# Four edits to the mixer of a hybrid decoder layer: dt in two stacked passes, v in blocks of 512 columns, norm sums as two halves times ones, the state matmul one projection later

## The chip, the cores and the metric

The kernel runs on one core of a Trainium2 chip, as one program that computes a whole decoder layer for one sequence of 256 tokens. The metric is the time of one execution in microseconds (us) on the device. The kernel before takes 869.53 us (median of three runs, 868.91 to 870.09).

## The reference

The layer has three parts in a row: a SwiGLU block, a mixer, and another SwiGLU block, each behind an RMS norm with a shift and a scale that come from a condition vector. The change is in the mixer alone. D is 1024, the sequence T is 256, a chunk is 128 tokens.

```
proj = u @ w_in        # one product for z, xbc, dt, q, k, v, g and two gates
# Mamba-2 (SSD) branch, 4 groups of 8 heads of 64
dt   = softplus(dt_raw + dt_bias)
y_diag = (cb * segsum_exp(a)) @ xdt
chunk_states = einsum(bm, decay_to_end, xdt)       # carried to the second chunk
y_off = cm @ prev_states * exp(a_cs)
yg = ((y_diag + y_off + xs * d_skip) * silu(z)) grouped in 4 groups of 512 channels
y_ssd = rms_normalize(yg) * norm_w                 # mean over 512 channels
# retention branch, 8 heads, key width 128, value width 256
y = ((q k^T) * decay_mask) @ v  (+ the part across chunks)
y_ret = rms_normalize(y) * norm_w * silu(g)        # mean over 256 channels
out = (sigmoid(gate_ssd) * (y_ssd @ w_br_ssd) + sigmoid(gate_ret) * (y_ret @ w_br_ret)) @ w_out
rms_normalize(x) = x * rsqrt(mean(x * x) + 1e-6)
```

## The kernel before

All data are float32, and a large product is made of reduced pieces. Every operand is split into two halves of type fp32r, a type that the tensor engine takes in one pass: hi is the value rounded to that type (a copy on ACT) and lo is what is left (a subtraction on DVE). A product is then three matmuls that add into one PSUM bank, hi·hi, hi·lo and lo·hi: the function `mm3`, lines 137 to 139, which holds most of the tensor engine's time. Small products are done in plain float32, without halves; each such matmul shows in the trace as two records (x2).

Weights come in pieces of 1 MB into four staging buffers (`wst`, filled by SP's DMA queue), are split by `half` (lines 128 and 129, ACT then DVE) into four pairs of buffers `wh` and `wl`, and are used once. Activations u of the layer stand in SBUF as `uh` and `ul`, features on the partitions, tokens along the free axis.

PSUM is used in two pools. **proj** has four banks of 128 x 512 float32, one for each projection under way; **misc** has the other four, for all small products. Nearly every projection takes one proj bank: two halves of 256 tokens, or, in v, two chunks of 128 tokens by 256 columns. A bank is given to the next tile in turn when its reader, a copy or activation on ACT or an addition on DVE, has emptied it.

The mixer is a list of steps, the string ORDER, and each step is one Python function: `dt`, `conv`, `states`, `mul`, `back`, `norma`, `normb`, `v`, `bs`, `rs`, `rv`, `rn` and so on, with the number of a group, tile or head behind the dot. The string sets the order in which the program is written, and that order sets which buffer a tile gets. A scheduler then orders the instructions of each engine by its own estimates of when their inputs are ready, so that small matmuls land among the projection's matmuls. On the chip each engine runs its own list in order and waits on semaphores.

What the change and the steps ahead speak of:

- `dt` (lines 524 to 534): the raw dt of 32 heads. The weights have only 32 columns, so that the 24 matmuls of `mm3` fill 32 of 128 output rows each. A copy on ACT (531) brings the sum to SBUF and two transposes (534) put tokens on the partitions.
- `states.g` (619 to 637): eight transposes (624) turn one group's channels, DVE multiplies them by dt (625, `xd`) and by the decay to the chunk's end (630, `xe`), and in the same step the state matmul (635) multiplies `xe` by `bn`; ACT copies the result to `st` (636). `back.g` (666 to 688) reads `xd`, the masks and `st`.
- The masks `m` of a group are filled by DMAs of POOL's queue (644, 647, step `ml.g`), which wait until `back` of an earlier group has read the buffers, and then by ACT (655, steps `ma.g` and `mb.g`).
- `norma.g` squares and adds (694 to 697), `normb.g` takes the mean over 512 channels in `rstd`: a matmul of a constant matrix filled with 1/512 and the sums, in plain float32 (line 205), and then logarithm, exponential and a correction step. `rn.h` of a retention head does the same with 1/256, after `rv.h` has made the values and their squares.
- `rv.h` (799 to 810): for each of two halves of a head's 256 columns three matmuls of 128 x 128 in plain float32: value chunk 0 with score columns of chunk 0 (804), the same with those of chunk 1 (805), and value chunk 1 (806), which adds to the latter.
- `v.p` (753 to 764), p from 0 to 7: 256 columns of v, with u as the stationary operand; for each chunk of 128 tokens 24 matmuls of 128 x 256 into one half of a proj bank. A copy on ACT (764) empties the bank.
- `bs.g.q` (713 to 731): the SSD branch's output product of a group, two proj banks for each q, which an ACT copy (729, group 0) or a DVE addition (731) empties.

Of the kernel before, what the change touches and what calls it, by code (L numbers as in the profile page):

```python
# [12 lines left out]
F32 = mybir.dt.float32  # L13
F32R = mybir.dt.float32r
# [4 lines left out]
P = 128  # L19
# [19 lines left out]
K_ID, K_TRI, K_M = 0, 128, 256  # L39
K_INV, K_SGN = 640, 641  # L40
N_CONST = 642

# [16 lines left out]
    "br.3.0 gr.1 br.3.1 ada ada gr.3 ada ada ada "  # L59
)  # L60


def constants():
    c = np.zeros((P, N_CONST), np.float32)
    i = np.arange(P)
    c[:, K_ID:K_ID + P] = np.eye(P)
    c[:, K_TRI:K_TRI + P] = i[:, None] <= i[None, :]
    for j, n in enumerate((1024, 512, 256)):
        c[:, K_M + j * P:K_M + (j + 1) * P] = 1.0 / n
    c[:, K_INV] = 10000.0 ** (-(i % 64) / 64.0)  # L70
    c[:, K_SGN] = np.where(i < 64, -1.0, 1.0)
    lg = np.log1p(-np.exp2(-5.0 - np.arange(8)))
    rel = np.arange(T)[None, :] - i[:, None]
    dm = np.where(rel >= 0, np.exp(lg[:, None, None] * np.maximum(rel, 0)), 0.0) * P ** -0.5
    dm = np.ascontiguousarray(dm.transpose(1, 0, 2).reshape(P, 8 * T)).astype(np.float32)
    return c, dm
# [3 lines left out]
def layer(ctx: ExitStack, tc: tile.TileContext, a, out, packing):  # L80
# [60 lines left out]
    def at(pair, *idx):  # L141
        return pair[0][idx], pair[1][idx]
# [8 lines left out]
    triu = k[:, K_TRI:K_TRI + P]  # L151
    mean_m = {n: k[:, K_M + j * P:K_M + (j + 1) * P] for j, n in enumerate((1024, 512, 256))}
    ones = cst.tile([P, P], F32, name="ones")
# [47 lines left out]

    def rstd(parts, n):
        ps = misc_ps()
        for i, s in enumerate(parts):
            pe.matmul(ps[:, :T], mean_m[n], s, start=i == 0, stop=i == len(parts) - 1)  # L205
        rs = sp.tile([P, T], F32, tag="rs", name=nm("rs"), bufs=2)
        t = sp.tile([P, T], F32, tag="rt", name=nm("rt"), bufs=2)
        lookup(rs, ps[:, :T], AF.Ln, bias=epsc)
        lookup(rs, rs, AF.Exp, scale=-0.5)
        dve.tensor_tensor(t, rs, rs, ALU.mult)  # L210
        dve.scalar_tensor_tensor(t, ps[:, :T], EPS, t, ALU.add, ALU.mult)
        dve.tensor_scalar(t, t, -0.5, 1.5, ALU.mult, ALU.add)
        dve.tensor_tensor(rs, rs, t, ALU.mult)
        return rs
# [30 lines left out]
    def modulated(ha, u, jsh, w, cols):  # L245
        rs = []
        ps = early_project(w, cols, u, 1, lambda: rs.append(rstd(sums, D)))
        rs = rs[0]
# [229 lines left out]
    with tc.tile_pool(name="mx", bufs=1, reuse_waits="tile") as mx:  # L478
# [9 lines left out]
        def wide(shape, dt=F32):  # L488
            return mx.tile(shape, dt, tag="m", name=nm("m"), bufs=WIDE_BUFS)
# [34 lines left out]
        def dt_tile():  # L524
            need("e")
            hv = half(load(w_in, 0, KD, C_DT, NH))
            ps = proj_ps()
            for kt in range(KD):
                mm3(ps[:NH, 0, :], at(hv, al, kt), at(u, al, kt), kt == 0, kt == KD - 1)
            dtr = wide([NH, T])  # L530
            act.copy(dtr, ps[:NH, 0, :])
            ps = misc_ps()
            for c in range(2):
                pe.transpose(ps[:, c * NH:(c + 1) * NH], dtr[:, c * P:(c + 1) * P],
                             ident[:NH, :NH])
            v, e, s1, s2, pl = (small([P, 2, NH], n) for n in ("dtv", "dte_", "dts", "dts2", "dtp"))
# [82 lines left out]
        def ssd_states(g):  # L619
            xd = slot([P, 2, 512])  # L620
            for c in range(2):
# [9 lines left out]
                xe.rearrange("p (h q) -> p h q", h=8), xd[:, 0, :].rearrange("p (h q) -> p h q", h=8),  # L631
                dend[:, 8 * g:8 * g + 8].unsqueeze(2).broadcast_to([P, 8, 64]), ALU.mult)
            st = small([P, 512], "st")
            ps = misc_ps()
# [54 lines left out]

        hls = {}  # L690

        def norm_a(g):
            y, sz = xs[g], zs["z", g]
            dve.tensor_tensor(y, y, sz, ALU.mult)
            act.activation(sz, y, AF.Square)
            dve.tensor_tensor(sz[:, 0:2, :], sz[:, 0:2, :], sz[:, 2:4, :], ALU.add)
            dve.tensor_tensor(sz[:, 0, :], sz[:, 0, :], sz[:, 1, :], ALU.add)

        def norm_b(g):
            need("e")  # L700
            y, sz = xs.pop(g), zs.pop(("z", g))
            rs = rstd([sz[:, 0, :]], 512)
            for f in range(4):
# [46 lines left out]

        vn = []

        def v_tile(p2):
            st = load(w_in, 0, KD, C_V + p2 * 256, 256)
            hv = [half(st[:, 4 * i:4 * i + 4, :]) for i in range(2)]
            ps = proj_ps()
            for c in range(2):
                ts = slice(c * P, (c + 1) * P)
                for kt in range(KD):
                    mm3(ps[:, c, :], at(u, al, kt, ts), at(hv[kt // 4], al, kt % 4),  # L760
                        kt == 0, kt == KD - 1)
            if p2 % 2 == 0:
                vn.append(slot([P, 2, 2, T]))
            act.copy(vn[-1][:, p2 % 2], ps)

# [33 lines left out]
        def ret_values(hd):  # L799
            sc, v = scs.pop(hd), vn[hd // 2][:, hd % 2]  # L800
            py = misc_ps().rearrange("p (e t) -> p e t", e=2)
            for eh in range(2):
                es = slice(eh * P, (eh + 1) * P)
                pe.matmul(py[:, eh, :P], v[:, 0, es], sc[:, :P], start=True, stop=True)
                pe.matmul(py[:, eh, P:], v[:, 0, es], sc[:, P:T], start=True, stop=False)
                pe.matmul(py[:, eh, P:], v[:, 1, es], sc[:, T:], start=False, stop=True)
            sq = mx.tile([P, 2, T], F32, tag="cv", name=nm("rsq"), bufs=2)
            act.activation(sq, py, AF.Square)
            dve.tensor_tensor(sq[:, 0, :], sq[:, 0, :], sq[:, 1, :], ALU.add)
            pys[hd] = py, sq  # L810

        def ret_norm(hd):
            need("e")
            py, sq = pys.pop(hd)
            rs = rstd([sq[:, 0, :]], 256)
            y = wide([P, 2, T])
# [14 lines left out]
            "g": lambda g, p2: silu_half(("g", g), C_G + g * 512, p2),  # L831
            "states": ssd_states, "ma": lambda g: ssd_masks(g, 0), "mb": lambda g: ssd_masks(g, 1), "ml": mask_rows,
            "mul": mask_scores, "back": ssd_back, "norma": norm_a,
# [159 lines left out]
```

## Time and profile before

The profiled execution took 870.23 us, at a mean granted TensorE clock of 0.996. Its span, from the first to the last instruction in the trace, is 868.4 us; the other 1.83 us lie around it.

| | before |
|---|---|
| median of 3 runs | 869.53 us (868.91 to 870.09) |
| profiled execution | 870.23 us |
| span of its trace | 868.4 us |
| data moved by DMA | 193.24 MB, mean 223 GB/s |
| casts of weights on ACT, line 128 | 282, 289.3 us busy |
| subtractions on DVE, line 129 | 282, 336.7 us busy |

A row of a timeline reads: start in us from the beginning of the span, busy time in us, engine, line of the kernel, operation, output<-inputs by the program's names, shapes and count, and in brackets the wait just before it and what ended it. Matmuls overlap in the array, so the cost of one in a stream is read from start to start and not from its busy time. PE is TensorE, DVE is VectorE, ACT is ScalarE, POOL is GpSimd.

### The profile page before, as it was taken

Reading aid. Unit: us, or ns where it says so; the run is one execution under the profiler, and the core shown is the slowest. Engines: PE = TensorE matmul, PEld = TensorE weight load, DVE = VectorE, ACT = ScalarE, POOL = GpSimd, SP = SyncE. Lnnn points to the kernel's source line nnn. Section 1 sums busy time; section 2 is a strip of 40 time slices with the busy share of each in tenths; the row PEclk is TensorE's granted clock in tenths of the full one; section 3 lists DMA queues with packets and bytes.
Section 4 is the critical chain, followed back from the end, with each engine's and each line's share of the span. In section 5 each row is a group of like instructions: output and inputs, shape, how many; then the busy total and the mean of one; then the engine's idle time right before and its main releaser. Section 6 shows DMA issues by size and latency. Waiting matters only on the chain.

```text
span 868.4 us, 16684 instructions
## 1 busy us (share of the span) xinstructions
PE 852.7 (98%) x6982; PEld 835.4 (96%) x6982; DVE 667.0 (77%) x1007; ACT 502.5 (58%) x709; POOL 10.3 (1%) x21
## 2 busy tenths in 40 slices
PE   7999999999999999999999999999999999999996
PEld 5999999999999998999999999999999999999896
DVE  6989798986889877788798677976979975455453
ACT  5454444465798686765464558755558644545342
POOL 0000000000100010000000000000000000000000
PEclk9999999999999999999999999999999999999999
DMA  9968878894595454445557664464554784455521
GB/s 362 414 223 334 275 275 321 338 366 183 183 335 193 177 177 176 182 146 178 211 188 276 223 235 159 170 243 146 204 216 171 266 330 172 170 172 180 185 95 48
DMA packets 30589, 193.24 MB, mean 223 GB/s; under 512 B 3489, under 2 KB 3873, under 8 KB 10802
## 3 DMA queue, kind: packets, MB, share of 16 engines
q1 hardware_dynamic: 28658, 186.47, 59.1%
q0 software_dynamic: 1568, 5.28, 1.8%
q8 instruction: 54, 0.88, 0.4%
q10 hardware_dynamic: 288, 0.44, 0.1%
q14 instruction: 21, 0.17, 0.1%
HBM read 191.09 MB, written 1.08 MB: 221 GB/s over the span
## 4 chain that ended last, share of the span: by engine, by line
PE 89%; DVE 5%; ACT 3%; DMA 2%; issue 1%; SPq 0%; DVEq 0%; ACTq 0%
PE proj L139 27%; PE proj L138 27%; PE proj L137 27%; DVE wl L129 2%; PE misc L137 1%; PE misc L139 1%; PE misc L138 1%; PE misc L674 1%; DMA wst<-in_ada_w_dram 1%; PE misc L205 1%; ACT wh L128 1%; DVE wst L181 1%; DMA ada<-in_ada_w_dram 1%; DMA wst<-in_ffn_w_out_dram 1%; PE misc L684 1%
## 5 line engine op out<-in xcount | busy, mean ns | idle before, releaser
L128 ACT CAST wh<-wst 128x1024 fp32r<-128x1024 f32 (+3 forms) x282 | 289.3, 1031 | 275.8 <-PE proj L138 185.4
L129 DVE TENSOR_TENSOR wl<-wst,wh 128x1024 fp32r<-128x1024 f32 (+3 forms) x282 | 336.7, 1200 | 135.4 <-ACT wh L128 134.9
L137 PE MATMUL proj<-uh,wh 128*128 128x256 f32 (+1 forms) x1336 | 376.8, 283 | 2.3 <-ACT uh L222 2.3
L139 PE MATMUL proj<-uh,wl 128*128 128x256 f32 (+1 forms) x1336 | 377.4, 283 | 0.8 <-DVE wl L129 0.8
L138 PE MATMUL proj<-ul,wh 128*128 128x256 f32 (+1 forms) x1336 | 375.8, 281 | 0.0
L137 PEld LDWEIGHTS proj<-uh,wh 128*128 128x128 f32 x1336 | 250.9, 188 | 3.0 <-ACT uh L222 2.5
L139 PEld LDWEIGHTS proj<-uh,wl 128*128 128x128 f32 x1336 | 252.3, 189 | 1.3 <-DVE wl L129 1.0
L138 PEld LDWEIGHTS proj<-ul,wh 128*128 128x128 f32 x1336 | 252.3, 189 | 0.5 <-issue 0.2
L137 PE MATMUL proj<-s,wh 128*128 128x256 f32 x320 | 90.0, 282 | 0.2 <-ACT s L133 0.2
L139 PE MATMUL proj<-s,wl 128*128 128x256 f32 x320 | 90.0, 282 | 0.0
L138 PE MATMUL proj<-s,wh 128*128 128x256 f32 x320 | 89.3, 280 | 0.0
L181 DVE SCALAR_TENSOR_TENSOR wst<-wst,cb 128x1024 f32<-128x1024 f32 x56 | 67.4, 1220 | 10.1 <-DMA wst<-in_ada_w_dram 10.0
L137 PEld LDWEIGHTS proj<-s,wh 128*128 128x128 f32 x320 | 60.0, 188 | 1.0 <-issue 0.5
L139 PEld LDWEIGHTS proj<-s,wl 128*128 128x128 f32 x320 | 60.1, 188 | 0.5 <-issue 0.5
L138 PEld LDWEIGHTS proj<-s,wh 128*128 128x128 f32 x320 | 60.2, 188 | 0.1
L139 PE MATMUL proj<-ah,wl 128*128 128x256 f32 x176 | 49.2, 280 | 0.2 <-DVE wl L129 0.2
L137 PE MATMUL proj<-ah,wh 128*128 128x256 f32 x176 | 49.1, 279 | 0.0
L138 PE MATMUL proj<-al,wh 128*128 128x256 f32 x176 | 49.1, 279 | 0.0
L138 PE MATMUL proj<-wl,ah 128*128 128x256 f32 (+1 forms) x132 | 42.1, 319 | 0.0
L139 PE MATMUL proj<-wh,al 128*128 128x256 f32 (+1 forms) x132 | 42.1, 319 | 0.0
L137 PE MATMUL proj<-wh,ah 128*128 128x256 f32 (+1 forms) x132 | 42.1, 319 | 0.0
L161 ACT ACT_TABLE_LOAD x30 | 38.5, 1283 | 1.2 <-PEq L966 0.7
(222 smaller groups left out, 1124.6 us busy)
## 6 DMA issues: line engine op xcount, KB each, us to landing
wst<-in_mix_w_in_dram SPq DMA_DIRECT2D x52, 1024.0 KB, 4.9
wst<-in_ffn_w_in_dram SPq DMA_DIRECT2D x37, 1024.0 KB, 5.1
wst<-in_ada_w_dram SPq DMA_DIRECT2D x28, 1024.0 KB, 5.6
wst<-in_ffn_w_out_dram SPq DMA_DIRECT2D x17, 1024.0 KB, 4.9
ada<-in_ada_w_dram SPq DMA_DIRECT2D x16, 512.0 KB, 12.0
wst<-in_w_br_ssd_dram SPq DMA_DIRECT2D x8, 1024.0 KB, 4.9
wst<-in_w_br_ret_dram SPq DMA_DIRECT2D x8, 1024.0 KB, 5.0
wst<-in_ffn_w_in_dram SPq DMA_DIRECT2D x7, 896.0 KB, 12.7
```

The source lines that it names most:

```text
L128: act.copy(hi, v)
L129: dve.tensor_tensor(lo, v, hi.bitcast(F32), ALU.subtract)
L137: pe.matmul(o, l[0], r[0], start=first, stop=False, skip_group_check=skip)
L138: pe.matmul(o, l[0], r[1], start=False, stop=False, skip_group_check=skip)
L139: pe.matmul(o, l[1], r[0], start=False, stop=last, skip_group_check=skip)
L161: ins = act.preload_act_table_set(name).ins
L181: dve.scalar_tensor_tensor(st[:, i, :], st[:, i, :], 1.0, cb, ALU.mult, ALU.mult, accum_out=raw[:, j, f0 + i:f0 + i + 1])
L205: pe.matmul(ps[:, :T], mean_m[n], s, start=i == 0, stop=i == len(parts) - 1)
L674: pe.matmul(py[hh * 64:hh * 64 + 64, f * T + c * P:f * T + (c + 1) * P], xd[:, c, hl * 64:hl * 64 + 64], m[c][:, hl, :], start=True, stop= ...
L684: pe.matmul(po[:, f * P:(f + 1) * P], st[:, f * P:(f + 1) * P], cT[:, g, P:], start=True, stop=True)
```

## The change

**dt.** The hi and lo halves of the 32 columns now lie side by side, 64 columns as one stationary operand. One matmul per block of 128 features multiplies both halves by `uh` and fills 64 output rows, a second one multiplies hi by `ul` into the first 32: 16 matmuls instead of 24. The two partial sums in rows 0 to 31 and 32 to 63 are added when they are turned: the two transposes become two matmuls with a 64 x 32 matrix `both`, two identities on top of each other, which one small DVE addition makes.

**v.** A step now takes four of the eight feature blocks of 512 columns instead of eight blocks of 256 columns: two proj banks, one per chunk of tokens, are held over two steps (even p starts the sums, odd p ends them), and a matmul is 128 x 512. The two copies follow the odd step.

**Norm sums.** `norma` and `rv` now also split the sums into halves, scaled by 1/n (`mean_halves`: ACT for hi, DVE for lo), and `normb` and `rn` multiply the two halves by a matrix of ones of type fp32r: two fp32r matmuls instead of one plain float32 matmul. The retention squares' buffer is free earlier; the halves have one buffer each.

**Values of the retention.** Lines 804 and 805 become one matmul of 128 x 256 that starts the sum, and 806 adds to its second half.

**State matmul.** It becomes a step of its own, `state.g`, written one projection later than `states.g`.

```diff
-    "conv.7 conv.5 conv.3 ma.0 bc v.0 mb.0 states.0 mul.0 v.1 back.0 ml.2 v.2 ma.1 v.3 states.1 "
-    "mb.1 norma.0 v.4 normb.0 mul.1 z.1.0 z.1.1 back.1 ml.3 states.2 bs.0.0 ma.2 norma.1 bs.0.1 "
+    "conv.7 conv.5 conv.3 ma.0 bc v.0 mb.0 states.0 mul.0 v.1 state.0 back.0 ml.2 v.2 ma.1 v.3 "
+    "states.1 mb.1 norma.0 v.4 state.1 normb.0 mul.1 z.1.0 z.1.1 back.1 ml.3 states.2 bs.0.0 state.2 "
...
-    mean_m = {n: k[:, K_M + j * P:K_M + (j + 1) * P] for j, n in enumerate((1024, 512, 256))}
+    mean_m = k[:, K_M:K_M + P]
...
-    def rstd(parts, n):
+    def rstd(parts, mean):
         ps = misc_ps()
         for i, s in enumerate(parts):
-            pe.matmul(ps[:, :T], mean_m[n], s, start=i == 0, stop=i == len(parts) - 1)
+            pe.matmul(ps[:, :T], mean, s, start=i == 0, stop=i == len(parts) - 1)
...
         def dt_tile():
             need("e")
-            hv = half(load(w_in, 0, KD, C_DT, NH))
+            st = load(w_in, 0, KD, C_DT, NH)
+            wd = wp.tile([P, 1024], F32R, tag="wh", name=nm("wh"), bufs=HALF_BUFS)
+            wd = wd[:, :KD * 2 * NH].rearrange("p (k n) -> p k n", k=KD)
+            split_into(wd[:, :, :NH], wd[:, :, NH:], st)
             ps = proj_ps()
             for kt in range(KD):
-                mm3(ps[:NH, 0, :], at(hv, al, kt), at(u, al, kt), kt == 0, kt == KD - 1)
-            dtr = wide([NH, T])
-            act.copy(dtr, ps[:NH, 0, :])
+                uh, ul = at(u, al, kt)
+                if kt:
+                    pe.matmul(ps[:NH, 0, :], wd[:, kt, :NH], ul, start=False, stop=False)
+                pe.matmul(ps[:2 * NH, 0, :], wd[:, kt, :], uh, start=kt == 0, stop=kt == KD - 1)
+                if not kt:
+                    pe.matmul(ps[:NH, 0, :], wd[:, kt, :NH], ul, start=False, stop=False)
+            both = small([2 * NH, NH], "both")
+            dve.tensor_tensor(both, ident[:2 * NH, :NH], ident[:2 * NH, NH:2 * NH], ALU.add)
+            dtr = wide([2 * NH, T])
+            act.copy(dtr, ps[:2 * NH, 0, :])
             ps = misc_ps()
             for c in range(2):
-                pe.transpose(ps[:, c * NH:(c + 1) * NH], dtr[:, c * P:(c + 1) * P],
-                             ident[:NH, :NH])
+                pe.matmul(ps[:, c * NH:(c + 1) * NH], dtr[:, c * P:(c + 1) * P], both,
+                          start=True, stop=True)
...
+            states[g] = xd, xe
+
+        def ssd_state(g):
+            xd, xe = states[g]
             st = small([P, 512], "st")
...
+        ones_r = mx.tile([P, P], F32R, tag="onesr", name="onesr", bufs=1)
+        act.copy(ones_r, ones)
+
+        def mean_halves(n, s):
+            hi, lo = (mx.tile([P, T], F32R, tag=t, name=nm(t), bufs=1) for t in ("sqh", "sql"))
+            act.activation(hi, s, AF.Copy, scale=1.0 / n)
+            dve.scalar_tensor_tensor(lo, s, 1.0 / n, hi.bitcast(F32), ALU.mult, ALU.subtract)
+            return hi, lo
...
+            halves["s", g] = mean_halves(512, sz[:, 0, :])
...
-            rs = rstd([sz[:, 0, :]], 512)
+            rs = rstd(halves.pop(("s", g)), ones_r)
...
         def v_tile(p2):
-            st = load(w_in, 0, KD, C_V + p2 * 256, 256)
-            hv = [half(st[:, 4 * i:4 * i + 4, :]) for i in range(2)]
-            ps = proj_ps()
+            k0 = p2 % 2 * 4
+            st = load(w_in, k0 * P, 4, C_V + p2 // 2 * 512, 512)
+            hv = [half(st[:, 2 * i:2 * i + 2, :]) for i in range(2)]
+            if k0 == 0:
+                v_ps[:] = [proj_ps() for _ in range(2)]
             for c in range(2):
-                ts = slice(c * P, (c + 1) * P)
-                for kt in range(KD):
-                    mm3(ps[:, c, :], at(u, al, kt, ts), at(hv[kt // 4], al, kt % 4),
-                        kt == 0, kt == KD - 1)
-            if p2 % 2 == 0:
+                ps = v_ps[c].rearrange("p d t -> p (d t)")
+                for kt in range(k0, k0 + 4):
+                    mm3(ps, at(u, al, kt, slice(c * P, (c + 1) * P)),
+                        at(hv[kt % 4 // 2], al, kt % 2), kt == 0, kt == KD - 1)
+            if k0:
                 vn.append(slot([P, 2, 2, T]))
-            act.copy(vn[-1][:, p2 % 2], ps)
+                for c in range(2):
+                    act.copy(vn[-1][:, :, c, :], v_ps[c])
...
-                pe.matmul(py[:, eh, :P], v[:, 0, es], sc[:, :P], start=True, stop=True)
-                pe.matmul(py[:, eh, P:], v[:, 0, es], sc[:, P:T], start=True, stop=False)
+                pe.matmul(py[:, eh, :], v[:, 0, es], sc[:, :T], start=True, stop=False)
                 pe.matmul(py[:, eh, P:], v[:, 1, es], sc[:, T:], start=False, stop=True)
...
-            pys[hd] = py, sq
+            pys[hd] = py, mean_halves(256, sq[:, 0, :])
```

In the change's own numbering `mm3` stands at lines 135 to 137, `half` at 126 and 127, the state matmul at 647 and its copy at 648, the masks at 667, `mean_halves` at 709 and 710, the norm matmul at 203, the branch's copy at 752, the values at 830 and 831.

First place, **PE around the state matmul of group 1**, while v.4 runs. In the program before the eight transposes of `states.1` (624) come first; `proj_462` is the bank of v.4 and `misc_456` the state:

```order
L624 MATMUL misc_452_3872<-k_72,s_365_3108 128x128 x4
L624 MATMUL misc_453_3878<-k_72,s_365_3108 128x128 x4
L137 MATMUL proj_462_3914<-wh_458_3906,uh_10_147 128x256
L138 MATMUL proj_462_3914<-wl_459_3907,uh_10_147 128x256
...
L139 MATMUL proj_462_3914<-wh_460_3910,ul_11_148 128x256
L137 MATMUL proj_462_3914<-wh_460_3910,uh_10_147 128x256
L635 MATMUL misc_456_3887<-xe_454_3884,bn_296_2592 128x512
L138 MATMUL proj_462_3914<-wl_461_3911,uh_10_147 128x256
```

The state matmul stands after 19 matmuls of v.4, and 29 more follow it. The same place on PE in the change, where v.4 fills two banks, `proj_462` and `proj_463`:

```order
L632 MATMUL misc_452_3771<-k_72,s_365_3103 128x128 x4
L632 MATMUL misc_453_3777<-k_72,s_365_3103 128x128 x4
L135 MATMUL proj_462_3813<-wh_458_3805,uh_10_147 128x512
...
L137 MATMUL proj_463_3814<-wh_460_3809,ul_11_148 128x512
L647 MATMUL misc_465_3840<-xe_454_3783,bn_296_2592 128x512
L203 MATMUL misc_466_3843<-sqh_455_3799,onesr_2595 128x256
L203 MATMUL misc_466_3843<-sql_456_3800,onesr_2595 128x256
L135 MATMUL proj_473_3868<-uh_10_147,wh_474_3869 128x256
```

All 24 matmuls of v.4, each twice as wide, now stand ahead of the state matmul, and the norm of group 0 is two matmuls behind it.

Second place, **ACT around the product bs.0.0**. Before, `m_487` is a mask of group 2, `proj_499` and `proj_502` are the two banks of bs.0.0, and `wh_511` holds the first weights of v.5:

```order
L169 ACTIVATE ec_435_3734<-ec_435_3734 128x512
L655 ACTIVATE m_487_4138<-m_487_4138,cs_297_2593 128x128 x4
L128 CAST wh_511_4314<-wst_510_4312 128x1024
L729 COPY s_494_4162<-proj_499_4170 128x512
L655 ACTIVATE m_487_4138<-m_487_4138,cs_297_2593 128x128
L636 COPY st_492_4158<-misc_493_4159 128x512
```

And in the change, where `m_489` is that mask and `wh_515` holds those weights:

```order
L167 ACTIVATE ec_435_3681<-ec_435_3681 128x512
L667 ACTIVATE m_489_4017<-m_489_4017,cs_297_2593 128x128 x4
L126 CAST wh_515_4197<-wst_514_4195 128x1024
L752 COPY s_494_4037<-proj_499_4045 128x512
L667 ACTIVATE m_489_4017<-m_489_4017,cs_297_2593 128x128
L716 ACTIVATE s_471_3865<-s_365_3103 128x1024
L667 ACTIVATE m_489_4017<-m_489_4017,cs_297_2593 128x128
L752 COPY s_494_4037<-proj_502_4075 128x512
```

The copies stand behind the same masks and cast as before. What moved is the bank that the next product needs: before, the four proj banks go round, and bs.0.1 takes the two that bs.0.0 did not use. In the change v.4 and v.5 hold two banks from v.4 to the end of v.5, and z.1.0, z.1.1, bs.0.0 and bs.0.1 between them share the other two, so that the first product of bs.0.1 (`proj_510`) takes the bank of `proj_499`.

Third place, **PE at the first retention heads**: rv.0, rs.1, the projection `proj_744` (g.1.0), rv.1 and the norm of head 0. Before:

```order
L805 MATMUL misc_730_6196<-m_716_6065,s_419_3612 128x128
L806 MATMUL misc_730_6196<-m_716_6065,s_419_3612 128x128
L792 MATMUL misc_732_6206<-s_618_5212,s_627_5282 128x256
L793 MATMUL misc_732_6206<-s_618_5212,s_627_5282 128x128
...
L805 MATMUL misc_734_6212<-m_733_6209,s_419_3612 128x128
L205 MATMUL misc_736_6223<-rsq_731_6203,k_72 128x256
L806 MATMUL misc_734_6212<-m_733_6209,s_419_3612 128x128
```

In the change, with `proj_756` for g.1.0 and `sqh_740` and `sql_741` for the halves of head 0's sums:

```order
L830 MATMUL misc_738_6019<-m_724_5888,s_429_3645 128x256
L831 MATMUL misc_738_6019<-m_724_5888,s_429_3645 128x128
L818 MATMUL misc_742_6031<-s_626_5035,s_635_5105 128x256
L819 MATMUL misc_742_6031<-s_626_5035,s_635_5105 128x128
...
L831 MATMUL misc_744_6037<-m_743_6034,s_429_3645 128x128
L203 MATMUL misc_748_6050<-sqh_740_6027,onesr_2595 128x256
L137 MATMUL proj_756_6073<-uh_10_147,wl_758_6075 128x256
...
L203 MATMUL misc_748_6050<-sql_741_6028,onesr_2595 128x256
```

The norm's one matmul, which stood among those of rv.1, is two now: that of the hi half right behind rv.1, that of the lo half nine matmuls of the projection later.

More of the change, by code (lines that the diff above doesn't have):

```diff
@@ L39 @@
 K_ID, K_TRI, K_M = 0, 128, 256
-K_INV, K_SGN = 640, 641
-N_CONST = 642
+K_INV, K_SGN = 384, 385
+N_CONST = 386
 STAGE_BUFS = 4
@@ L50 @@
     "dt z.0.0 decays ml.0 ml.1 conv.8 conv.4 conv.10 conv.0 conv.1 conv.9 conv.2 conv.11 conv.6 "
[8 rows of a table removed]
-    "br.3.0 gr.1 br.3.1 ada ada gr.3 ada ada ada "
[8 rows of a table added]
 )
@@ L67, in constants @@
     c[:, K_TRI:K_TRI + P] = i[:, None] <= i[None, :]
-    for j, n in enumerate((1024, 512, 256)):
-        c[:, K_M + j * P:K_M + (j + 1) * P] = 1.0 / n
+    c[:, K_M:K_M + P] = 1.0 / D
     c[:, K_INV] = 10000.0 ** (-(i % 64) / 64.0)
@@ L246, in modulated @@
         rs = []
-        ps = early_project(w, cols, u, 1, lambda: rs.append(rstd(sums, D)))
+        ps = early_project(w, cols, u, 1, lambda: rs.append(rstd(sums, mean_m)))
         rs = rs[0]
@@ L688, in ssd_back @@
                               ec.rearrange("p (f l) -> p f l", f=4), ALU.add)
-        hls = {}
+        hls, halves = {}, {}
+        ones_r = mx.tile([P, P], F32R, tag="onesr", name="onesr", bufs=1)
[5 more added lines that the diff above has]
+            return hi, lo
         def norm_a(g):
@@ L697, in norm_a @@
             dve.tensor_tensor(sz[:, 0, :], sz[:, 0, :], sz[:, 1, :], ALU.add)
+            halves["s", g] = mean_halves(512, sz[:, 0, :])
         def norm_b(g):
             need("e")
-            y, sz = xs.pop(g), zs.pop(("z", g))
-            rs = rstd([sz[:, 0, :]], 512)
+            y = xs.pop(g)
+            zs.pop(("z", g))
+            rs = rstd(halves.pop(("s", g)), ones_r)
             for f in range(4):
@@ L749, in gate_ssd @@
                 dve.tensor_tensor(totals["s"][q], totals["s"][q], gates["s"][q], ALU.mult)
-        vn = []
+        vn, v_ps = [], []
         def v_tile(p2):
-            st = load(w_in, 0, KD, C_V + p2 * 256, 256)
-            hv = [half(st[:, 4 * i:4 * i + 4, :]) for i in range(2)]
-            ps = proj_ps()
-            for c in range(2):
-                ts = slice(c * P, (c + 1) * P)
-                for kt in range(KD):
-                    mm3(ps[:, c, :], at(u, al, kt, ts), at(hv[kt // 4], al, kt % 4),
-                        kt == 0, kt == KD - 1)
-            if p2 % 2 == 0:
+            k0 = p2 % 2 * 4
[3 more added lines that the diff above has]
+                v_ps[:] = [proj_ps() for _ in range(2)]
+            for c in range(2):
+                ps = v_ps[c].rearrange("p d t -> p (d t)")
[3 more added lines that the diff above has]
+            if k0:
                 vn.append(slot([P, 2, 2, T]))
-            act.copy(vn[-1][:, p2 % 2], ps)
+                for c in range(2):
+                    act.copy(vn[-1][:, :, c, :], v_ps[c])
         def rotary(c0, dst):
@@ L809, in ret_values @@
             dve.tensor_tensor(sq[:, 0, :], sq[:, 0, :], sq[:, 1, :], ALU.add)
-            pys[hd] = py, sq
+            pys[hd] = py, mean_halves(256, sq[:, 0, :])
         def ret_norm(hd):
             need("e")
-            py, sq = pys.pop(hd)
-            rs = rstd([sq[:, 0, :]], 256)
+            py, hl = pys.pop(hd)
+            rs = rstd(hl, ones_r)
             y = wide([P, 2, T])
@@ L831, in layer @@
             "g": lambda g, p2: silu_half(("g", g), C_G + g * 512, p2),
-            "states": ssd_states, "ma": lambda g: ssd_masks(g, 0), "mb": lambda g: ssd_masks(g, 1), "ml": mask_rows,
+            "states": ssd_states, "state": ssd_state,
+            "ma": lambda g: ssd_masks(g, 0), "mb": lambda g: ssd_masks(g, 1), "ml": mask_rows,
             "mul": mask_scores, "back": ssd_back, "norma": norm_a,
```

12 rows, old and new, of the table ORDER are left out of this document.

## The prediction

> **What bounds the kernel now.** I read the page's head first, then the chain of work that ended last, then TensorE's waits.
>
> ```profile
> span 868.4 us, 16684 instructions
> PE 852.7 (98%) x6982; PEld 835.4 (96%) x6982; DVE 667.0 (77%) x1007; ACT 502.5 (58%) x709; POOL 10.3 (1%) x21
> PE 89%; DVE 5%; ACT 3%; DMA 2%; issue 1%; SPq 0%; DVEq 0%; ACTq 0%
> ```
>
> TensorE (PE) is busy for 98% of the span and makes 89% of the chain. The profiled execution took 870.23 us, 1.83 more than its span, at a granted clock of 0.996. PE's waits, the longest by line:
>
> ```profile
> PE misc L362 <- DMA crow<-in_c_dram: 2.5, 1, 2.5
> PE proj L137 <- ACT uh L222: 2.3, 1, 2.3
> PE misc L635 <- DVE xe L630: 1.2, 1, 1.2
> PE proj L139 <- DVE wl L129: 1.0, 2, 0.8
> ```
>
> The columns are total us, count and longest. Only the third lies in the mixer on a line that the change moves. So PE's own work can shrink almost one for one, and a new wait on PE costs its full length; DVE and ACT count only where they make PE wait. A change of 0.2% (1.7 us) is about what a measurement of this kernel can tell from none.
>
> **Norm sums.** One plain float32 matmul becomes two fp32r ones. The group norm in TensorE's timeline:
>
> ```profile
> 332.82 0.28 PE L139 MATMUL proj<-wh,ul 128*128 128x256 f32 x1
> 332.94 0.59 PE L205 MATMUL misc<-s,k 128*128 128x256 f32 x2
> 333.18 0.47 PE L137 MATMUL proj<-uh,wh 128*128 128x256 f32 x1
> 333.49 0.28 PE L138 MATMUL proj<-ul,wh 128*128 128x256 f32 x1
> ```
>
> L205 and the L137 behind it take 333.49 - 332.94 = 0.55 us from start to start, of which an fp32r matmul of 128x256 is 0.12 (332.82 to 332.94). So the float32 sum costs 0.43, two fp32r ones 0.24, and 0.195 is saved at each of 12 norms (4 SSD groups, 8 heads): **-2.35 us**. The three norms over 1024 keep their matmul. The new ACT scaling and DVE subtraction lie beside PE's work; their price is under the waits.
>
> **v.** 384 matmuls of 128x256 become 192 of 128x512. The first and the last of 47 successive ones of a v tile, and of 26 wide ones in the last projection:
>
> ```profile
> 318.56 0.28 PE L138 MATMUL proj<-wl,uh 128*128 128x256 f32 x1
> ...
> 324.01 0.28 PE L139 MATMUL proj<-wh,ul 128*128 128x256 f32 x1
> ...
> 799.94 0.40 PE L138 MATMUL proj<-wl,ah 128*128 128x512 f32 x1
> ...
> 805.78 0.40 PE L139 MATMUL proj<-wh,al 128*128 128x512 f32 x1
> ```
>
> 5.45 / 46 = 0.1185 us against 5.84 / 25 = 0.2336: two narrow ones 0.237, one wide 0.2336, a saving of 0.0034 times 192, **-0.65 us** (0.3 to 1.0 with the rounding of the rows).
>
> The Trainium skill (TensorE: Matmul & The Clock Gate, section Back-to-back issue gap) gives a sustained 131 ns for a matmul with 512 columns, and N / 2.4 + 2.5 ns for an isolated one. By the first, v would lose some (0.237 - 0.131) x 192 = 20 us; by the second, 2.5 ns a pair, 0.5 us. The wide rows above, 0.2336 us in a full stream of this number type, disagree with the first and leave it no chance; the second is of the size that I take.
>
> **dt.** 24 matmuls that fill 32 output rows each become 16. Rows in time order, with ACT's copy and PE's transposes behind it, and two of the float32 matmuls of the decays:
>
> ```profile
> 220.93 0.28 PE L137 MATMUL proj<-uh,wh 128*32 128x256 f32 x1
> ...
> 223.62 0.28 PE L139 MATMUL proj<-uh,wl 128*32 128x256 f32 x1
> 224.83 0.35 ACT L531 COPY m<-proj 32x256 f32<-32x256 f32 x1
> 224.92 0.28 PE L138 MATMUL proj<-ul,wh 128*128 128x256 f32 x1
> 225.24 0.31 PE L534 MATMUL misc<-k,m 32*128 32x32 f32 x2
> 225.47 0.39 PE L139 MATMUL proj<-uh,wl 128*128 128x256 f32 x1
> ...
> 231.11 0.63 PE L605 MATMUL misc<-av,k 128*128 128x32 f32 x4
> 231.58 0.39 PE L608 MATMUL misc<-av,ones 128*128 128x32 f32 x2
> ```
>
> 2.69 / 23 = 0.117 a piece with 32 columns, no cheaper than with 128, so 64 columns will not cost more either: 8 x 0.117 = 0.94 saved. The two transposes take 225.47 - 225.24 = 0.23; as plain matmuls they are two records each, like the L605 pair (four records, 231.58 - 231.11 = 0.47): 0.24 added. Ahead of L534 PE stood about 0.2 us (224.92 + 0.117 to 225.24) for the copy; the same wait stays (0 to 0.5, since fewer matmuls are put behind the copy's source). The addition for `both` is 32 columns on DVE long before. **-0.65 us**.
>
> **Values of the retention.** Six plain float32 matmuls become four, two of them 256 wide (L792 is that shape):
>
> ```profile
> 524.15 0.38 PE L804 MATMUL misc<-m,s 128*128 128x128 f32 x2
> ...
> 525.49 0.60 PE L792 MATMUL misc<-s,s 128*128 128x256 f32 x2
> 525.92 0.38 PE L793 MATMUL misc<-s,s 128*128 128x128 f32 x2
> ```
>
> L804 to L792 is 1.34 us for six; L792 costs 0.43 (525.92 - 525.49). After it is 2 x 0.43 + 2 x 0.223 = 1.31: 0.03 a head, **-0.27 us** for eight.
>
> **State matmul.** The chain's own rows, and PE around it:
>
> ```profile
> 325.42 1.23 DVE wl L129
> ...
> 327.76 0.69 DVE xe L630
> 328.59 1.10 PE misc L635 x2
> ...
> 327.14 0.28 PE L137 MATMUL proj<-wh,uh 128*128 128x256 f32 x1
> 328.59 1.10 PE L635 MATMUL misc<-xe,bn 128*128 128x512 f32 x2 [1.17 <-DVE xe L630]
> ```
>
> PE starts L137 at 327.14 and then stands until 328.59 for `xe`, which DVE had behind a weight half. 1.45 less L137's own 0.12 is 1.33 us of idle time. In the change the state matmul of that group stands behind all of v.4, which PE leaves near 330.6 in this time frame (29 matmuls of 0.1185 behind the 327.14 row), 2 us after `xe` is there: **-1.33 us**. The other groups show no such wait, so for them it is nothing. `st` is copied later on ACT, for `back.g` some microseconds on; it is the next thing that could be late, by my count with half a microsecond to spare at group 0.
>
> **What is added: a bank wait.** v.4 and v.5 hold two proj banks while z.1.0, z.1.1, bs.0.0 and bs.0.1 run, so bs.0.1 begins in the bank of the first half of bs.0.0. That bank is emptied by ACT's copy, behind a mask row that waits for its DMA and behind a weight cast:
>
> ```profile
> 347.38 0.56 POOL L644 DMA_DIRECT2D m<-rows  x1 [30.46 <-ACT s L169]
> 353.84 1.28 ACT L655 ACTIVATE m<-m,cs 128x128 f32<-128x128 f32 x4 [3.28 <-DMA m<-rows]
> 355.03 1.04 ACT L128 CAST wh<-wst 128x1024 fp32r<-128x1024 f32 x1
> 355.97 0.57 ACT L729 COPY s<-proj 128x512 f32<-128x512 f32 x1
> 354.66 0.28 PE L137 MATMUL proj<-s,wh 128*128 128x256 f32 x1
> ...
> m<-rows POOLq DMA_DIRECT2D x8, 512.0 KB, 8.2
> ```
>
> The last timeline row is where bs.0.1 begins. The copy ends at 356.54; PE wants the bank at 354.66. That is **+1.9 us** on PE, with all of bs.0.1, v.5 and what follows behind it in PE's list. Bounds: nothing, if the mask's DMA lands 2 us sooner than its 6.5 (347.38 to 353.84), and about 3.5 if it lands as late as the median of these transfers, 8.2 by the row of issues (operation, count, size, median us to landing). Then everything on PE moves together, so it is not made up later. The second half of bs.0.1 would want its bank 2.8 us after the first, and that copy follows on ACT within it: no more. For v.6 and v.7 the branch's banks are emptied by DVE additions without a DMA ahead; no wait.
>
> A rule speaks against this part: the Trainium skill (Perfetto Trace Analysis, section Matmuls) wants independent groups of matmuls to go round the PSUM banks, so that emptying one lies beside the next. Its sum is my +1.9; without it v is a plain gain. In the trace of before no bank wait shows among PE's longest.
>
> **Other waits.** At the first retention norms the sums pass through ACT once more, where casts stand:
>
> ```profile
> 526.61 0.60 ACT L808 ACTIVATE rsq<-misc 128x512 f32<-128x512 f32 x1
> 527.11 1.98 ACT L128 CAST wh<-wst 128x1024 fp32r<-128x1024 f32 x2
> 527.72 0.70 PE L205 MATMUL misc<-rsq,k 128*128 128x256 f32 x2 [0.19 <-DVE rsq L809]
> ```
>
> Before, PE waits 0.19 there, behind DVE's addition. In the change the hi half follows a cast of 1 us on ACT, ready near 528.5, while PE wants it near 528.15: some 0.4. The lo half, ready near 529.6, has nine projection matmuls ahead of it (1.05 us). Later heads stand deeper among projections. I take **+0.3 us** in all (-0.2 to +1.5, the latter three norms of 0.5).
>
> **Sum:** -2.35 - 0.65 - 0.65 - 0.27 - 1.33 + 1.9 + 0.3 = -3.05 us: 870.2 to 867.2 profiled. That execution lies 0.7 above the median of the runs, so the forecast is 869.5 - 3.05 = **866.5 us**.
>
> **Rivals.**
> - *No bank wait.* The mask lands sooner, or the copy comes ahead on ACT: 866.5 - 1.9 = 864.6. For it: DMA time varies (the row above is under the median). Against it: the mask is asked for only after POOL's 30.46 us wait, and ACT's list keeps the copy behind it. 0.17.
> - *Longer waits.* The mask lands as late as the median (+1.7), or half a microsecond more at several retention norms: 867.7 to 869.5. 0.20.
> - *Slower: the hi halves queue behind casts.* Each of the 8 retention norms waits about a microsecond for ACT, a cast's length by the 1.98 for two: +8 - 3.05, about 874.5. It decides where PE has under 1 us of other matmuls between the values and their sum. For it: the 527.11 row stands exactly there. Against it: PE's list has nine projection matmuls ahead of the lo half even at the first head, and ACT is at 58%. 0.06.
> - *It does not do what it says.* Two fp32r matmuls with a fresh weight each cost as much as the float32 sum, which is two records too: -2.35 goes, 868.8. Against it: 0.118 us in every fp32r stream above. 0.05.
>
> **Numbers.** The forecast, 865.5 to 867.7 by itself, 0.52. The range, 8 times in 10, takes in the second and most of the third: 863.8 to 869.2. Faster by over 0.2% (below 867.8): the forecast, the first rival and a little of the second, 0.73. Within 0.2%: the rest of the second, the last and a sliver of the forecast, 0.21. Slower: 0.06.
>
> **What would show it.** Lines here are those of the change's own numbering. TensorE's list has some 200 matmuls fewer. The pairs at L203 take 0.24, wide rows of v 0.233 from start to start, the two matmuls at L542 0.47. L647 shows no wait. The first L135 of bs.0.1 waits about 1.9 us for ACT's copy at L752, and it is the longest wait of the mixer. The clock stays at 1.00. I am wrong if L203 waits for L709 or L710 by more than half a microsecond at several heads, if a copy of v or `st` (L648) makes PE wait, or if the weights' halves come late because ACT and DVE have more to do.

## The result and the profile after

The changed kernel takes 863.70 us (median of six runs, 863.12 to 864.84) against 869.50 us (six runs, 868.91 to 870.09): a ratio of 0.9928, 95% interval 0.9912 to 0.9944. It is 5.8 us faster where 3.05 was forecast, just outside the range (863.8 to 869.2). The profiled execution took 864.84 us, with a span of 863.1, of which TensorE is busy for 847.8 (98%) with 6752 matmul records, 230 fewer than before. TensorE's waits in the change (total us, count, longest):

```profile
...
PE misc L382 <- DVE modc L396: 1.8, 1, 1.8
PE proj L135 <- ACT s L752: 0.8, 1, 0.8
...
PE misc L203 <- ACT sqh L709: 0.2, 1, 0.2
```

The first row, and the two longer ones left out above it, belong to the first 20 us of the program. TensorE still bounds the kernel. Beside the rows of before, three things are to be seen: the wait for `xe` (1.2) is gone, the wait for the branch's copy (line 752) is there but with 0.8 us instead of the 1.9 of the forecast, and the row `PE proj L139 <- DVE wl L129`, 1.0 us in two waits, which the prediction had shown and set aside, is gone too.

To see where the time went, cut the program at places that both lists of TensorE share: at its 301st matmul record (49.09 us before, 49.78 after), at the mixer's first norm sum, and at the first norm sum of the second SwiGLU block. Windows of the kernel before (stretch, its length, then the busy time of PE, of its weight loads, DVE, ACT and POOL, the clock, DMA share and GB/s):

```profile
49.09:209.92 160.83, 159.87 (x1352) 159.46 (x1351) 134.04 (x204) 81.16 (x111) 0.00 (x0) 1.00 0.78 285
209.92:670.01 460.09, 458.43 (x3871) 452.10 (x3869) 373.82 (x571) 303.52 (x446) 10.10 (x17) 1.00 0.56 200
```

The same two stretches of the change:

```profile
49.78:209.11 159.33, 159.33 (x1353) 159.33 (x1351) 134.24 (x204) 82.18 (x111) 0.00 (x0) 1.00 0.78 287
209.11:664.61 455.50, 454.28 (x3641) 439.06 (x3639) 377.47 (x584) 309.53 (x459) 10.14 (x17) 1.00 0.57 202
```

Read the first number behind the stretch. The mixer gained 4.59 us. The first SwiGLU block, where no line was edited, gained 1.50. Behind the mixer, up to the start of the last matmul, the two agree within 0.02 us (190.93 and 190.95), and ahead of the 301st record this execution of the change lost 0.69; over the twelve profiles that record starts anywhere from 47.76 to 49.78. So the forecast has two errors: a gain outside the mixer that it did not have, and 1.5 us too little inside. The clock is 1.00 in all four rows.

### The first SwiGLU block

TensorE's wait at 61 us in the kernel before, and ACT and DVE ahead of it:

```profile
56.37 1.20 ACT L169 ACTIVATE s<-proj 128x512 f32<-128x512 f32 x2 [2.66 <-PE proj L139]
57.47 1.99 ACT L128 CAST wh<-wst 128x1024 fp32r<-128x1024 f32 x2
...
58.48 1.29 DVE L300 TENSOR_TENSOR s<-s,proj 128x512 f32<-128x512 f32 x2 [3.65 <-PE proj L139]
59.69 1.22 DVE L129 TENSOR_TENSOR wl<-wst,wh 128x1024 fp32r<-128x1024 f32 x1
...
60.96 0.38 PE L139 MATMUL proj<-uh,wl 128*128 128x256 f32 x1 [0.79 <-DVE wl L129]
```

And in the change, where TensorE does not wait there:

```profile
57.06 0.60 ACT L167 ACTIVATE s<-proj 128x512 f32<-128x512 f32 x1 [2.54 <-PE proj L137]
57.55 1.04 ACT L126 CAST wh<-wst 128x1024 fp32r<-128x1024 f32 x1
58.49 0.60 ACT L167 ACTIVATE s<-proj 128x512 f32<-128x512 f32 x1
...
58.63 1.23 DVE L127 TENSOR_TENSOR wl<-wst,wh 128x1024 fp32r<-128x1024 f32 x1 [2.98 <-ACT wh L126]
```

Before, ACT does both activations and then the weight cast, so that DVE has the low weight half only behind two products, at 60.91. In the change the cast stands between the activations, and the low half is there at 59.86. No line of this block was edited, but the change is not in the mixer alone: the constants table, whose transfer runs from 34 to 47 us, just ahead of this stretch, shrank from 642 to 386 columns with the two matrices of the mean. The lines (`N_CONST`) do not stand in the diff above; experiment 2 shows them. With the table's size, so the idea that experiments 1 and 2 try, the scheduler's estimates changed, and with them the order of ACT and DVE here.

### The wait for the bank

ACT and TensorE around the start of bs.0.1 in the change:

```profile
349.47 1.28 ACT L667 ACTIVATE m<-m,cs 128x128 f32<-128x128 f32 x4 [3.16 <-DMA m<-rows]
350.36 1.02 PE L647 MATMUL misc<-xe,bn 128*128 128x512 f32 x2
350.66 1.03 ACT L126 CAST wh<-wst 128x1024 fp32r<-128x1024 f32 x1
351.60 0.57 ACT L752 COPY s<-proj 128x512 f32<-128x512 f32 x1
352.22 0.39 PE L135 MATMUL proj<-s,wh 128*128 128x256 f32 x1 [0.84 <-ACT s L752]
```

The chain is the one that was forecast: mask rows, weight cast, copy, and the first matmul of bs.0.1 starts as the copy ends at 352.17. From the mask rows to the end of the copy it takes 2.70 us, as before (353.84 to 356.54). What was wrong is when TensorE wants the bank. Between the two products stands the state matmul of group 2, 0.86 us (two records that start 0.43 apart). Before, it stood inside bs.0.0:

```profile
352.28 1.02 PE L635 MATMUL misc<-xe,bn 128*128 128x512 f32 x2
...
355.36 0.28 PE L137 MATMUL proj<-s,wh 128*128 128x256 f32 x1
```

Counted from the start of bs.0.0 at 348.80, the second row is the 49th matmul of the branch and so the first of bs.0.1. The row at 354.66, which the prediction took for it, is the 43rd. With 355.36 the same rows give 356.54 - 355.36 = 1.2 us.

### State, norm and v

TensorE at the state matmul of group 1 and the norm of group 0, with the last matmul of v.4 ahead of them:

```profile
328.11 0.40 PE L137 MATMUL proj<-wh,ul 128*128 128x512 f32 x1
328.34 1.02 PE L647 MATMUL misc<-xe,bn 128*128 128x512 f32 x2
328.80 0.69 PE L203 MATMUL misc<-sqh,onesr 128*128 128x256 f32 x1
329.32 0.28 PE L203 MATMUL misc<-sql,onesr 128*128 128x256 f32 x1
329.44 0.28 PE L135 MATMUL proj<-uh,wh 128*128 128x256 f32 x1
```

No wait stands at L647. State and norm together take 329.44 - 328.34 = 1.10 us, and before the state alone, with its wait, took 2.26 more than the stream and the norm 0.43. Of the 1.10 the state is 0.86, so the pair of fp32r sums costs 0.24, as forecast. The wide matmul of v ahead of them takes 328.34 - 328.11 = 0.23 from start to start.

For the experiments below the table gives the same stretches. "Mixer" is the window from the mixer's first norm sum to that of the second SwiGLU block, "block 1" from the 301st record to the mixer. The medians also hold the start of the program, which differs by up to 2 us between the profiles; the stretches leave it out. They come from one profile each: block 1 repeats to 0.01 us in eight kernels, but the mixer of the change differs by 0.2 between the change and e1, and that of before by 0.4 between before and e2, so smaller differences in that column tell nothing. The runs came in four batches, and the ratio is to the kernel before in the same batch, whose median was 869.50 with the change, 869.76 with e1 to e4, 869.86 with e5 to e8 and 870.45 with e9 and e10.

| kernel | median us (runs) | ratio to before, interval | block 1 | mixer |
|---|---|---|---|---|
| before | 869.50 (6) | | 160.83 | 460.09 |
| change | 863.70 (6) | 0.9928, 0.9912 to 0.9944 | 159.33 | 455.50 |
| e1 change, constants 510 wide | 864.42 (5) | 0.9936, 0.9922 to 0.9949 | 160.39 | 455.70 |
| e2 before, constants 386 wide | 868.79 (11) | 0.9985, 0.9976 to 0.9994 | 160.12 | 460.46 |
| e3 change, lo first | 863.38 (5) | 0.9924, 0.9912 to 0.9937 | 159.33 | 455.73 |
| e4 change, bs.0.1 behind v.5 | 862.74 (5) | 0.9915, 0.9902 to 0.9927 | 159.33 | 454.46 |
| e5 change, v of 256 | 863.90 (6) | 0.9931, 0.9918 to 0.9944 | 159.33 | 455.62 |
| e6 change, float32 norm sums | 865.46 (5) | 0.9948, 0.9934 to 0.9961 | 159.33 | 456.95 |
| e7 change, state not moved | 866.26 (6) | 0.9957, 0.9943 to 0.9970 | 159.33 | 457.56 |
| e8 change, dt as before | 865.39 (6) | 0.9949, 0.9932 to 0.9966 | 159.33 | 456.49 |
| e9 as e4, two buffers for halves | 862.75 (5) | 0.9918, 0.9904 to 0.9932 | 159.33 | 453.87 |
| e10 before, v of 512 | 869.53 (11) | 0.9998, 0.9988 to 1.0009 | 161.02 | 460.47 |

### The profile page after: what moved, and what is told of

It reads as the page before. It is cut to its first block, busy times and chain, and to the rows that moved or that the text cites. A ratio compares the mean times of both kernels' runs of the same rounds, so it can differ in the third digit from the quotient of the medians.

```text
span 863.1 us, 16252 instructions
## 1 busy us (share of the span) xinstructions
PE 847.8 (98%) x6752; PEld 822.1 (95%) x6752; DVE 670.6 (78%) x1020; ACT 509.2 (59%) x722; POOL 10.3 (1%) x21
## 4 chain that ended last, share of the span: by engine, by line
PE 88%; issue 4%; DVE 3%; ACT 2%; DMA 2%; SPq 0%; DVEq 0%; ACTq 0%; POOLq 0%
PE proj L137 27%; PE proj L135 27%; PE proj L136 27%; PE misc L135 1%; PE misc L137 1%; PE misc L136 1%; DVE wl L127 1%; DMA ada<-in_ada_w_dram 1%; ACT wh L126 1%; DMA m<-rows 1%; PE misc L686 1%; PE misc L830 1%; PE misc L203 1%; DVE ada L179 0%; PE misc L696 0%
```

## The experiments

**1. The size of the constants table.** In the change:

```diff
-K_INV, K_SGN = 384, 385
-N_CONST = 386
+K_INV, K_SGN = 508, 509
+N_CONST = 510
```

> The changed kernel with its constants table widened from 386 to 510 columns (the added columns are zeros and unused). This makes the scheduler order ACT's and DVE's work at the second input tiles of the first SwiGLU block as in the kernel before (activation ahead of the weight cast), and leaves TensorE's order as in the change. Theory: the wait of TensorE for line 127 (a weight half) near 61 us comes back, 0.8 to 1.0 us, and perhaps the 0.4 us one at 183 us: 864.6 to 865.2 us against 863.7 for the change. Rival: what the change gained ahead of the mixer was the luck of one execution's transfers: 863.7, and no wait for line 127 near 61 us.

TensorE's wait is back, and ACT does both activations ahead of the casts again:

```profile
55.21 1.20 ACT L167 ACTIVATE s<-proj 128x512 f32<-128x512 f32 x2 [1.42 <-PE proj L137]
56.30 1.99 ACT L126 CAST wh<-wst 128x1024 fp32r<-128x1024 f32 x2
...
59.80 0.38 PE L137 MATMUL proj<-uh,wl 128*128 128x256 f32 x1 [0.79 <-DVE wl L127]
```

Block 1 is 160.39 against 159.33, 1.06 us more, and the mixer is the change's within 0.2. The median rose by 0.7, a little less than expected. The wait at 183 us did not come back.

**2. The other way round, in the kernel before.**

```diff
-K_INV, K_SGN = 640, 641
-N_CONST = 642
+K_INV, K_SGN = 384, 385
+N_CONST = 386
...
+        for n in (512, 256):
+            mean_m[n] = mx.tile([P, P], F32, name=f"mean{n}")
+            dve.memset(mean_m[n], 1.0 / n)
```

> The kernel before, with only the constants table cut to 386 columns; the two matrices of 1/512 and 1/256 that it loses are filled by DVE at the start of the mixer. Theory: it gains 1.0 to 1.5 us ahead of the mixer, 868.0 to 868.5 against 869.5, and its waits no longer list line 129 near 61 us. Rival: no gain, 869.5.

The median fell by 1.0 us within its batch (869.76 to 868.79), and the interval excludes no gain. The wait at 61 us is gone, and ACT casts between the two activations, at 56.53, as in the change. The wait near 183 us stays, with 0.5 instead of 0.2. So the table's size alone moves block 1, by 1.06 us in the change and by 0.71 in the kernel before, and the order of ACT and DVE goes with it.

**3. The halves in the other order.** The change's `mean_halves` returns `lo, hi`:

```diff
-            return hi, lo
+            return lo, hi
```

> The changed kernel with the two halves of the norm sums given to the matmul in the other order, lo first. Theory: a sum's matmul that stands alone among the projection's matmuls shows its weight load (0.22 to 0.30 us each instead of 0.12), because its input comes just as TensorE reaches it; with lo first both halves are there when the first of them starts, so the two stand together and cost 0.24 in all. The retention norms that are split now (0.44 to 0.53 us) become 0.24: 0.6 to 1.0 us less in all, 862.7 to 863.1. Rival: TensorE then waits for the later half, and nothing is gained: 863.7, with waits for line 710.

This came from the change's trace at the norms of heads 6 and 7. TensorE's weight loads (PEld), its matmuls and ACT there:

```profile
599.74 0.19 PEld L203 LDWEIGHTS misc<-sqh,onesr 128*128 128x128 f32 x1
599.86 0.28 PE L203 MATMUL misc<-sqh,onesr 128*128 128x256 f32 x1
...
600.88 0.41 ACT L709 ACTIVATE sqh<-rsq 128x256 fp32r<-128x256 f32 x1
601.35 0.19 PEld L203 LDWEIGHTS misc<-sqh,onesr 128*128 128x128 f32 x1
601.35 0.38 PE L203 MATMUL misc<-sqh,onesr 128*128 128x256 f32 x1
...
602.63 0.38 PE L203 MATMUL misc<-sql,onesr 128*128 128x256 f32 x1
602.85 0.28 PE L136 MATMUL proj<-s,wh 128*128 128x256 f32 x1
```

Head 6 has its weights loaded 0.12 us ahead of its matmul, beneath the matmul in front. Head 7's halves come just as TensorE gets there (601.29 for hi): load and matmul start at the same time, and the next matmul starts 0.22 us later instead of 0.12 (602.63 to 602.85). With the waits, the two lone sums of head 7 cost 0.53, more than the 0.43 of the float32 sum. With lo first, the pair does stand together in this kernel:

```profile
601.02 0.39 PE L203 MATMUL misc<-sql,onesr 128*128 128x256 f32 x1
601.24 0.28 PE L203 MATMUL misc<-sqh,onesr 128*128 128x256 f32 x1
```

But TensorE waits for it, and the pair again costs 0.54. The mixer is 455.73, no better than 455.50: the rival was right. Order is not the matter; the halves come late. Experiment 9 follows from this.

**4. bs.0.1 behind v.5.**

```diff
-    "ma.2 norma.1 bs.0.1 mb.2 v.5 normb.1 ...
+    "ma.2 norma.1 mb.2 v.5 bs.0.1 normb.1 ...
```

> The changed kernel with the step bs.0.1 moved behind v.5, so that both banks of v are emptied before bs.0.1 takes its banks. Theory: the wait of TensorE for ACT's copy at line 752, 0.84 us idle and 1.1 us with the exposed weight load, goes: 862.6. Rival: v.5 takes the place of bs.0.1 in front of the same masks and the wait turns up on another line or on the later group norm: 863.7 or more.

As the theory had it: no wait at line 752 is listed, the mixer is 454.46, 1.04 us less, and the median is 862.74.

**5. v in blocks of 256 columns.** `v_tile` of the kernel before in the change, with its own bank for each step.

> The changed kernel with v in blocks of 256 columns, as before. Theory: v's wide matmuls save 0.65 us and their two held banks cost 1.1 us by the wait at line 752, so going back gains 0.4: 863.3, and no wait at line 752. Rival: the wide blocks save more than the stream's spacing says (fewer weight loads, other copies): 864.3 or more.

Median 863.90 and mixer 455.62, between theory and rival and level with the change. The wait at line 752 is gone. Since e4, also without the wait, has 454.46, wide blocks save 1.16 us, not the 0.65 of the sum, and the wait takes 1.04 of it back. The rows of v agree: undisturbed neighbours start 0.2316 us apart on average in e4 (179 pairs of wide ones) and 0.1187 in e5 (372 pairs of narrow ones), and 192 x (2 x 0.1187 - 0.2316) is 1.1.

**6. Norm sums in plain float32.**

```diff
-            act.activation(hi, s, AF.Copy, scale=1.0 / n)
-            dve.scalar_tensor_tensor(lo, s, 1.0 / n, hi.bitcast(F32), ALU.mult, ALU.subtract)
-            return hi, lo
+            return [s]
...
-            rs = rstd(halves.pop(("s", g)), ones_r)
+            rs = rstd(halves.pop(("s", g)), mean_s[512])
```

> The changed kernel with the norm sums of the SSD groups and the retention heads as one plain float32 matmul again (matrices of 1/512 and 1/256 filled by DVE; no halves). Theory from the trace of the change: 0.2 us at each of 4 SSD norms, and 0.85 in all at the retention norms, where halves that come just in time show their weight loads: 1.65 us slower, 865.4. Rival, the term as forecast: 12 x 0.195 = 2.35 us, 866.1.

865.46, and 1.45 us more in the mixer: near the theory's 1.65, not the 2.35.

**7. The state matmul not moved.**

```diff
-    ... states.0 mul.0 v.1 state.0 back.0 ...
+    ... states.0 state.0 mul.0 v.1 back.0 ...
```

and the same for the other three groups.

> The changed kernel with each state.g straight behind its states.g in the order string. TensorE's list then has the state matmul of group 1 behind 12 wide matmuls of v.4 (2.80 us) where the kernel before had 19 narrow ones (2.25). Theory: the wait for xe comes back but for that difference, 1.4 - 0.55 = 0.85 us: 864.5. Rivals: all of it, 865.1; or nothing, 863.7, if DVE has xe earlier in the change.

The mixer is 2.06 us longer, more than every case. TensorE's waits in this kernel:

```profile
PE proj L135 <- ACT s L752: 1.4, 2, 0.8
...
PE misc L647 <- DVE xe L638: 0.7, 1, 0.7
```

Its timeline on ACT, around the second copy of bs.0.0:

```profile
353.40 0.56 ACT L648 COPY st<-misc 128x512 f32<-128x512 f32 x1
...
355.41 1.04 ACT L126 CAST wh<-wst 128x1024 fp32r<-128x1024 f32 x1
356.35 0.57 ACT L752 COPY s<-proj 128x512 f32<-128x512 f32 x1
```

The wait for `xe` is as the theory had it. New is the second wait at line 752: with the state matmul early, ACT's list has the copy of `st` ahead of the second copy of bs.0.0, and a mask row and a weight cast too, and the second half of bs.0.1 waits as well. In the change that copy stands ahead of them and ends at 354.19.

**8. dt as before**, the lines of `dt_tile` taken back.

> The changed kernel with dt as before: 24 matmuls of 32 columns and two transposes. Theory: 0.68 us slower by the matmuls and transposes, and 0.2 more in the decays behind it: 864.4 to 864.6. Rival: the gain of 0.9 seen between the end of the first block and the B/C products is not dt's, 863.7.

The mixer is 0.99 us longer. The median, 865.39, is 1.7 above the change's, more than expected, with runs from 863.86 to 867.57. In the traces of both, the matmuls and their transposes account for 0.68 and the decays behind them for 0.22 (1.63 against 1.41 beside the stream).

**9. Two buffers for the retention halves**, on e4.

```diff
+            if tag:
+                both = mx.tile([P, 2, T], F32R, tag=tag, name=nm("sqb"), bufs=1)
+                hi, lo = both[:, 0, :], both[:, 1, :]
...
-            pys[hd] = py, mean_halves(256, sq[:, 0, :])
+            pys[hd] = py, mean_halves(256, sq[:, 0, :], ("xe", "st")[hd % 2])
```

The SSD groups keep the old buffers.

> The kernel of e4 (bs.0.1 behind v.5), and the halves of the retention sums in two buffers that take turns (space of xe and st, idle by then) instead of one. Theory: the sums of heads 5 and 7 are split because their one buffer is held until the norm of the head ahead of them has read it, so that their halves come late; with two buffers both pairs stand together, 0.24 instead of 0.51 to 0.54 us each: 0.5 less than e4 in the mixer, 862.2. Rival: as in e3 the pair waits where it stands and nothing is gained: 862.7.

At heads 6 and 7 all four sums now stand in one row:

```profile
596.50 0.64 PE L203 MATMUL misc<-sqb,onesr 128*128 128x256 f32 x4
596.98 0.28 PE L135 MATMUL proj<-s,wh 128*128 128x256 f32 x1
```

0.48 us for four, where heads 6 and 7 took 0.24 and 0.53 in the change. The mixer is 453.87, 0.59 less than e4 and 1.63 less than the change. The medians of e4 and e9 (862.74, 862.75) do not tell the two apart, and their intervals overlap that of the change; by the stretches of one profile each they are the two best.

**10. v of 512 alone, in the kernel before.**

> The kernel before with v alone in blocks of 512 columns over two held banks. Theory: v's matmuls save 1.1 us (e5 against e4) and a wait for ACT's copy of the first half of bs.0.0 costs some 1.2 (in the kernel before that copy ends at 356.54 and bs.0.1 begins at 355.36, counted through by matmuls): within 0.3 us of the kernel before, with that wait in TensorE's list. Rivals: the wait comes only with the other edits, 868.7; or it is the 1.9 us of the forecast, 870.6.

No change in time, ratio 0.9998 (0.9988 to 1.0009). TensorE's waits in this kernel:

```profile
PE proj L137 <- ACT s L729: 1.6, 2, 0.9
```

There are two waits for the branch's copies, as in e7 and for the same reason: the state is not moved here either. The mixer, 460.47, is that of e2 within 0.01 and 0.38 longer than that of before: v alone loses what it saves.

## Why the prediction was too small

**What stayed outside the sum.** The step that failed is "only the third lies in the mixer on a line that the change moves", by which the row of line 129, 1.0 us, was set aside. The sum had nothing for this row, and the runs showed 1.5 us: the diff cut a table, that moved ACT's order in a block nobody edited, and the longer of the row's two waits went, which is worth 1.06 us by e1. The other wait, of 0.2 to 0.5 us near 183 us, is found in all three kernels with the mixer of before and in none of the nine others, and block 1 is 0.4 to 0.8 us longer there; the order of ACT and DVE ahead of it is the same in e2 as in the change, but DVE's work that waits for transfers there runs some 3 us ahead in the change (a piece that DVE takes at 176.11 in e2 is taken at 173.06). Why is open. Without the 1.5 us the time would have come out near 865.2, inside the range, although the mixer's gain too was half as large again as the forecast.

**The bank wait** was right in kind, place and releaser, and mis-sized: +1.9 forecast, 1.04 by e4. The step that failed is "the last timeline row is where bs.0.1 begins"; the begin was 0.70 us later. The rule of the Trainium skill (Perfetto Trace Analysis, section Matmuls), that independent groups should rotate through PSUM banks, is borne out by e4 and e5: the held banks take back 1.04 of the 1.16 us that the larger matmuls give. In numbers, the step from 1.9 to 1.2 us is that begin; the last 0.2 was not followed. That the second half does not wait held, but only because of the state's move (e7, e10), which the prediction did not see.

**v**, -0.65 forecast, is -1.16 (e5 against e4). The price per matmul was right to 1%, but the term is a small difference of two large ones, and the failing step is to take the wide price from another projection: 0.2316 us in v's own rows instead of 0.2336 is 0.4 of it, and 0.1187 instead of 0.1185 for the narrow ones most of the rest. The sustained 131 ns for 512 columns of the Trainium skill (TensorE: Matmul & The Clock Gate, section Back-to-back issue gap) does not show in v either, which takes 232 ns.

**The state**, -1.33 forecast, is -1.40 where it stands (2.26 to 0.86). Undone in the change it costs 2.06, since the second bank wait comes with it (e7: 0.7 for `xe` and 0.6 for the second copy, by the list of waits).

**Norm sums**, -2.35 and +0.3 of waits forecast, are -1.45 (e6). At the SSD groups it is 0.20 each, as worked out. At the retention heads the listed wait is 0.15, at the first head, not half a microsecond at several, but the failing step is the price of 0.24 for halves that come late. At heads 5 and 7, where they come late because one buffer serves all heads (e9), the two sums gained nothing. At head 0 they took 0.76 with the wait, against 0.44 for the one float32 sum in e6. Standing apart costs nothing by itself: the sums of head 2, at 540.38 and 541.66, came in time and took 0.21. Nor did the slower rival come: no norm waited a microsecond.

**dt**, -0.65 forecast, is -0.99: its own work as forecast (-0.68) and 0.22 in the decays behind it, which the sum did not have. **The values**, -0.27, were not tried alone; two heads take 2.62 instead of 2.68 us, 0.24 for eight.

Undone one at a time, norms, dt, state and v cost 1.45 + 0.99 + 2.06 + 0.12 = 4.62 us, 4.86 with the values, and the whole change gained 4.59 in the mixer: the two bank waits connect state and v, so the parts do not simply add. Added up as they stand in the change, norms -1.45, dt -0.99, state -1.40, v -1.16, values -0.24 and the bank wait +1.04 make -4.20; the 0.4 left over was not traced, and is as much as the mixer differs between before and e2.

## What to carry to other kernels

Where a scheduler orders the work by estimates, compare the order of every engine over the whole program, also where the diff touches nothing; a row of waits is not safe from a change because its line was not edited. Before a new wait is priced, count the instructions from a sure mark to the one that will wait. An operation split in two pays only if each part is ready before the engine reaches it: look at how many buffers their inputs have.

## What was unexpected of the hardware

A matmul whose input arrives just as TensorE reaches it costs its successor the hidden weight load: 0.22 us from start to start instead of 0.12, with no wait of that length listed. And the first 50 us differ between executions of nearly the same instructions by up to 2 us (the 301st matmul record starts at 47.76 us in e9 and at 49.78 in the change), as much as several of the edits here are worth.
